# A one-core two-block model: the state-space layer's output projection laid between its last steps, a shorter softplus, first loads in three parts, and another order of routing and tail

## The chip, the cores and the metric

The kernel runs as one program on one core of a Trainium2 chip. The metric is the device time of an execution in microseconds (us). Four engines compute: TensorE (PE in the rows; weight loads are PEld), VectorE (DVE), ScalarE (ACT) and GpSimd (POOL). SyncE (SP) mostly issues DMA transfers.

## The reference

The input is one sequence of 256 tokens with 1024 features. Everything is float32. Only the parts around the change are shown.

```python
# block 1, layer 0: state-space mixer (32 heads in 8 groups, chunks of 64)
zxbcdt = u @ w_in;  z, xbc, dt_raw = split(zxbcdt);  xbc = silu(causal_conv(xbc) + conv_b)
dt = softplus(dt_raw + dt_bias);  a = -exp(a_log)
y = ssd_scan(xh * dt, dt * a, B, C) + xh * d_skip          # decays come from cumulative sums of dt*a
yg = (y * silu(z)) per group;  yg = yg * rsqrt(mean(yg**2) + eps) * norm_w
h = layer_norm(alpha * x + yg @ w_out)                      # the output projection
# then: squared-relu MLP, stick-breaking attention, MLP
# block 2: h = rms_norm(x, norm1_w) * (1 + sc1) + sh1;  x = x + g1 * token_mixer(h)   (softplus again, 8 columns)
h = rms_norm(x, norm2_w) * (1 + sc2) + sh2
comb = top-1 group of 4, top-2 experts of 8 in it           # routing over 32 experts
y = sum over experts of comb_e * (silu(h @ w_gate_e) * (h @ w_up_e)) @ w_down_e
x = x + g2 * y
return rms_norm(x, final_norm_w)
```

## The kernel before

The 256 tokens are two halves `m` of 128. Every large product is made of three matmuls on operands that are split into a rounded high part and a low part (`whi`, `wlo` for weights, `yh`, `yl` for activations). A weight comes by DMA in blocks of 1 MB (`wraw`); `wsplit` makes `whi` on ACT (L207) and `wlo` on DVE, now and then on POOL (L208). All matmuls of the helper `mm` stand under its one line, L233, so they are told apart by tiles. A scheduler orders the instructions of each engine, except inside `manual_schedule`, where the order of the code holds.

**State-space layer** (`mamba`). For each of 8 groups `g`, `proj(g)` makes the projections (tile `pj`), and `ssd(g)` is a generator of steps: `cb`, `xt` and `xdt`; two steps of decay weights (tile `bc`, read back by a DMA from `csd`); `spread`, which starts the next group's `bc` DMA; then `yp` on TensorE, `yz` on DVE (L474), `yz*Zg` on POOL (L476), the square on ACT and a sum `Zg` on POOL (L479); then `ss` on TensorE, `rr` on DVE (L485) and a power on POOL (L486); then `rb` on TensorE, `yz` on DVE (L492), `yh` on ACT and `yl` on DVE (L494). Steps of group g-1 and g-2 run between the projections of group g. Group 7 has no projections behind it. The output projection follows: 8 blocks `b` of `w_ao` (tile `acc`, four PSUM banks, 24 matmuls for each block). Block b needs the `yh`, `yl` of group b alone. Six blocks are issued in `phase_mamba`, the last two in `finish_ln`. In the code the blocks stand behind the last steps of groups 6 and 7, and the scheduler moves some of the matmuls up.

**Start.** `xT` and the first weight block come in four parts of 256 KB each; `dt_chain` computes softplus on 64 columns on DVE (L265 to L276), from which `cs`, the cumulative sums, and then `csT`, `csd` and the first `bc` follow.

**Routing** (`Router`). `logits(m)` (`lgp`), `route(m)` (a chain of small DVE operations from `lg` to `sel`), `split(m)` (the high and low part of the normalized rows, the low one by a POOL subtraction, L1474), `place(m)` (`pos`), `onehot`, `gather0` (`xgp`).

**Experts.** 96 blocks of 1 MB (`eraw`) stream through 18 buffers, issued by SP as buffers come free. For each k: `gu` (gate and up), `aT`, `down` (`py`, and its two parts `yh`, `yl`), `combine` (`yacc`). The last k ends the kernel: `grows` makes rows of g2 and of the final weight by 16 transposes (tile `rows`), then `final` scales, adds, squares, normalizes and writes the output.

Of the kernel before, what the change touches and what calls it, by code (L numbers as in the profile page):

```python
# [10 lines left out]
F32 = mybir.dt.float32  # L11
# [45 lines left out]
def lay(i):  # L57
# [60 lines left out]
    a["pv"] = pv  # L118
    a["c"] = f(i["c_2"])
# [40 lines left out]
def build(tc, A, out, dbg=None):  # L160
# [3 lines left out]
    with ctx:  # L164
# [97 lines left out]
        def softplus(dst, u, e, s_, q):  # L262
# [93 lines left out]
        def phase_mamba():  # L356
            with tc.tile_pool(name="mamba", bufs=2, reuse_waits="tile") as work:
                with tc.tile_pool(name="psm", bufs=4, space=PSUM, reuse_waits="tile") as psm:
                    yh, yl = mamba(work, psm)
                    acc = [pst("acc") for _ in range(4)]  # L360
                    for b in range(6):
                        tm(acc, wsplit(A["w_ao"][b]), yh, yl, 2 * b, b == 0, False)
                    return finish_ln(acc, [(wsplit(A["w_ao"][b]), yh, yl, 2 * b) for b in (6, 7)], 0)

        def mamba(work, psm):
# [10 lines left out]
            for c in range(0, 8, 2):  # L376
                cs, ws = slice(c, c + 2), slice(256 * c % 1024, 256 * c % 1024 + 512)
                with ExitStack() as es:
# [3 lines left out]
                    with tc.issue_after(x0):  # L382
                        tail = nc.sync.dma_start(raw0[:, 256 * c:256 * c + 512], A["w_a"][0][:, 256 * c:256 * c + 512]).ins
                S.activation(xh[:, cs], xT[:, cs], AF.Copy)
                V.tensor_tensor(xl[:, cs], xT[:, cs], xh[:, cs], op=OP.subtract)
                h, l = hl0[c // 4]
                S.activation(h[:, ws], raw0[:, 256 * c:256 * c + 512], AF.Copy)  # L387
                V.tensor_tensor(l[:, ws], raw0[:, 256 * c:256 * c + 512], h[:, ws], op=OP.subtract)
# [107 lines left out]
            rest = []  # L496
            for k, _ in enumerate(proj(0)):
                if k == 1:
                    dt_chain()
            rest.pop()()  # L500
            bcs = {(0, j): spread(work, 32, 2 * j, 2, 4) for j in range(2)}
# [3 lines left out]
            for g in range(1, 9):  # L505
                pr = proj(g) if g < 8 else iter(())
                sd = ssd(g - 1)
# [7 lines left out]
            for _ in range(3):  # L515
                next(old, 0)
            return yh, yl
# [4 lines left out]
        def brow(src, name, pool=None, q=nc.scalar):  # L522
            r = (pool or lnp_box[-1]).tile([128, D], F32, name=name, tag=name, bufs=1)
# [383 lines left out]
        def phase_mixer(keep, hT):  # L907
            gates = [keep.tile([128, 8, T], F32, name="gates", tag=t) for t in ("gA", "gB")]
            with wsp_pool(4, "right") as w_:
# [6 lines left out]
                with tc.tile_pool(name="mixo", bufs=2, reuse_waits="tile") as work, \  # L916
                        tc.tile_pool(name="pso", bufs=4, space=PSUM, reuse_waits="tile") as psd:
                    rt = mixer_out(keep, small, work, psd, *mhl[:2])
                    rt.early = mhl[2]
                    return raw2, rt  # L920
# [391 lines left out]
        def mixer_out(keep, small, work, psd, mh, ml):  # L1312
# [55 lines left out]
            def logits(m):  # L1368
                for c in range(8):
# [18 lines left out]
            rt.split(0, work, "hr")  # L1388
            add(1, 0, t)
            wo(1, 1, range(4))  # L1390
            rt.place(0)
            turn(1, 0, t)
            add(1, 1)

            def last(pool):
                junk = pool.tile([128, 512], F32, name="junk", tag="oc", bufs=1)
                turn(1, 1, junk)
                logits(1)
                route(1)
                rt.split(1, pool, "oT")  # L1400
# [6 lines left out]
        class Router:  # L1407
            def __init__(self, keep, bl):
# [17 lines left out]
                V.tensor_scalar(pn[:, 2:3], pn[:, 1:2], -2.0, 1.0, op0=OP.mult, op1=OP.add)  # L1426
                V.scalar_tensor_tensor(pn[:, 3:4], pn[:, 1:2], -64.0, pn[:, 0:1], op0=OP.mult, op1=OP.add)
                self.r, self.hs = [None, None], [None, None]
# [38 lines left out]
            def split(self, m, pool, tag):  # L1467
                h = self.hs[m]
# [384 lines left out]
```

## Time and profile before

| | before |
|---|---|
| median of 3 runs | 1240.29 us (1238.09 to 1243.02) |
| the profiled execution | 1241.94 us, span 1240.2 us |
| TensorE busy | 1181.6 us (95%) |
| VectorE busy | 757.1 us (61%) |
| ScalarE busy | 554.4 us (45%) |
| GpSimd busy | 215.7 us (17%) |
| mean granted TensorE clock | 0.983 |
| read from HBM | 293.38 MB, 239 GB/s over the span |

The shares are means over stages with different limits. Starts in the rows below are counted from the start of the span.

### The profile page before, as it was taken

To read this page: it belongs to the slowest core of one execution; us is meant where nothing else is said; L and a number is where in the kernel's file an instruction comes from. 1 tells how busy PE (TensorE), PEld (TensorE's weight loads), DVE (VectorE), ACT (ScalarE), POOL (GpSimd) and SP (SyncE) were. 2 spreads that over 40 slices of the span, in tenths; PEclk is the share of its full clock that TensorE was granted. 3 is DMA by queue.
4 is the path that set the end of the run, shared out by engine and by line. 5 is a ranking of instruction groups with operands and counts; after the bars stand their busy time and mean duration, and the time that the engine had idled before them with its cause. 6 is when DMAs were issued, how large, how long until landed. Compare 5 with 4: busy or idle time off the path is not lost. (4 is left out here: it accounts for less than half of the span.)

```text
span 1240.2 us, 19177 instructions
## 1 busy us (share of the span) xinstructions
PE 1181.6 (95%) x7669; PEld 966.7 (78%) x7669; DVE 757.1 (61%) x1241; ACT 554.4 (45%) x910; POOL 215.7 (17%) x164
## 2 busy tenths in 40 slices
PE   8799996999999999999999998999999989999995
PEld 7799995889899889978999987998999853444332
DVE  5878877497777675559777766667455772111113
ACT  4577573354444455646544434554444431111112
POOL 3355543000000000000000043355431020000001
PEclk9899999999999999999999999899999999999998
DMA  8655634547887744324878753443325599999992
GB/s 325 220 187 196 221 128 146 206 175 282 311 312 285 253 170 170 137 101 158 330 282 300 276 201 118 163 170 103 103 69 204 232 388 407 421 422 421 421 421 108
DMA packets 47078, 295.84 MB, mean 239 GB/s; under 512 B 5256, under 2 KB 6533, under 8 KB 14469
## 3 DMA queue, kind: packets, MB, share of 16 engines
q1 hardware_dynamic: 41120, 277.91, 59.6%
q10 hardware_dynamic: 5860, 16.63, 3.9%
q8 instruction: 62, 1.02, 0.3%
q14 instruction: 36, 0.29, 0.1%
HBM read 293.38 MB, written 2.71 MB: 239 GB/s over the span
## 5 line engine op out<-in xcount | busy, mean ns | idle before, releaser
L208 DVE TENSOR_TENSOR wlo<-wraw,whi 128x1024 fp32r<-128x1024 f32 x240 | 303.1, 1278 | 146.4 <-ACT whi L207 145.5
L207 ACT ACTIVATE whi<-wraw 128x1024 fp32r<-128x1024 f32 x282 | 294.0, 1057 | 212.0 <-PE acc L233 65.4
L208 POOL TENSOR_TENSOR wlo<-wraw,whi 128x1024 fp32r<-128x1024 f32 x42 | 109.8, 2622 | 265.6 <-ACT whi L207 265.6
L233 PE MATMUL u<-hTh,whi 128*128 128x256 f32 x448 | 125.7, 281 | 0.0
L233 PE MATMUL u<-hTh,wlo 128*128 128x256 f32 x448 | 125.3, 280 | 0.0
L233 PE MATMUL u<-hTl,whi 128*128 128x256 f32 x448 | 125.2, 280 | 0.0
L233 PE MATMUL pj<-xh,whi 128*128 128x256 f32 x384 | 113.2, 295 | 6.4 <-ACT whi L387 5.3
L233 PE MATMUL gu<-eraw,xg 128*64 128x512 f32 x512 | 113.3, 595 | 1.1 <-PE xgp L233 0.6
L233 PE MATMUL acc<-whi,mh 128*128 128x512 f32 x288 | 113.8, 395 | 0.0
L233 PE MATMUL pj<-xh,wlo 128*128 128x256 f32 x384 | 110.6, 288 | 3.3 <-DVE wlo L208 3.2
L233 PE MATMUL acc<-whi,ml 128*128 128x512 f32 x288 | 112.7, 391 | 0.0
L233 PE MATMUL acc<-wlo,mh 128*128 128x512 f32 x288 | 112.3, 390 | 0.0
L233 PE MATMUL pj<-xl,whi 128*128 128x256 f32 x384 | 110.8, 289 | 0.3
L233 PE MATMUL pj<-hTh,whi 128*128 128x256 f32 x320 | 93.4, 292 | 0.0
L233 PE MATMUL pj<-hTh,wlo 128*128 128x256 f32 x320 | 91.1, 285 | 0.0
L233 PE MATMUL pj<-hTl,whi 128*128 128x256 f32 x320 | 91.0, 284 | 0.0
L233 PEld LDWEIGHTS gu<-eraw,xg 128*64 128x64 f32 x512 | 36.9, 137 | 66.7 <-issue 62.5
L233 PEld LDWEIGHTS u<-hTh,whi 128*128 128x128 f32 x448 | 84.1, 188 | 1.7 <-issue 0.6
L233 PEld LDWEIGHTS u<-hTl,whi 128*128 128x128 f32 x448 | 83.9, 187 | 1.1
L233 PEld LDWEIGHTS u<-hTh,wlo 128*128 128x128 f32 x448 | 84.4, 188 | 0.0
L233 PEld LDWEIGHTS pj<-xh,whi 128*128 128x128 f32 x384 | 75.3, 196 | 8.8 <-ACT whi L387 5.3
L233 PEld LDWEIGHTS pj<-xh,wlo 128*128 128x128 f32 x384 | 75.5, 197 | 3.9 <-DVE wlo L208 3.4
(450 smaller groups left out, 2386.6 us busy)
## 6 DMA issues: line engine op xcount, KB each, us to landing
wraw<-in_w_dram SPq DMA_DIRECT2D x64, 1024.0 KB, 5.0
eraw<-in_w_gu_dram SPq DMA_DIRECT2D x58, 1024.0 KB, 19.3
eraw<-in_w_dn_dram SPq DMA_DIRECT2D x30, 1024.0 KB, 19.8
wraw<-in_w_mod_dram SPq DMA_DIRECT2D x24, 1024.0 KB, 6.0
wraw<-in_w_a_dram SPq DMA_DIRECT2D x23, 1024.0 KB, 5.3
wraw<-in_w_ao_dram SPq DMA_DIRECT2D x8, 1024.0 KB, 5.0
wraw<-in_w_bg_dram SPq DMA_DIRECT2D x8, 1024.0 KB, 5.1
bc<-csd ACTq DMA_DIRECT2D x16, 384.0 KB, 5.7
```

What stands on the lines that cost most here:

```text
L207: his.append(S.activation(h, r[:, us], AF.Copy).ins)
L208: (G if u in pool else V).tensor_tensor(l, r[:, us], h, op=OP.subtract)
L233: return PE.matmul(o, a, b, start=start, stop=stop, skip_group_check=True).ins
```

## The change

Six edits are made at once.

1. `mamba` returns the unfinished generators of groups 6 (`old`) and 7 (`sd`), and `phase_mamba` runs their steps between halves of blocks, `unit(b, m)` with 12 matmuls each, in an order written by hand for TensorE.
2. `softplus` takes one operation for a step of its polynomial, not two: seven fewer in each of the two places.
3. The first loads come in parts of 2, 2 and 4 of the 8 chunks. The sums `cs` and the first `spread` are called from the loop of group 1, and the first steps of group 0 start one projection later.
4. `split` is gone: `high` writes the high part straight from ACT, `low` makes the low part by one DVE operation. `logits(1)` comes in two halves, `gather0` takes all high parts before the low ones.
5. g2 is multiplied in `down` (now `chunk`), which gets one DVE operation more on its way and reads g2 from a row loaded by DMA.
6. `grows` and the POOL additions are gone. The final weight is loaded by DMA behind the last expert weights. The last `down` comes in chunks of 512, 256 and 256 columns with the sums of the final norm between them, `combine(6)` is wholly ahead of it, and the second half of the output is issued by ACT.

```diff
-                    yh, yl = mamba(work, psm)
+                    yh, yl, old, sd = mamba(work, psm)
                     acc = [pst("acc") for _ in range(4)]
-                    for b in range(6):
-                        tm(acc, wsplit(A["w_ao"][b]), yh, yl, 2 * b, b == 0, False)
+                    hl = {}
+                    def unit(b, m):
+                        if b not in hl:
+                            hl[b] = wsplit(A["w_ao"][b])
+                        tm(acc, hl[b], yh, yl, 2 * b, b == 0, False, mt=(m,))
+                    with tc.manual_schedule(engines={PE.engine}):
+                        for step in (sd, (0, 0), sd, (0, 1), old, sd, (1, 0), sd, old, (1, 1), sd, (2, 0), (2, 1),
+                                     (3, 0), sd, (3, 1), (4, 0), sd, (4, 1), (5, 0), (5, 1)):
+                            unit(*step) if isinstance(step, tuple) else next(step, 0)
...
-            V.tensor_scalar(q, e, 1.0 / (2 * K + 1), 1.0 / (2 * K - 1), op0=OP.mult, op1=OP.add)
+            V.tensor_scalar(q, e, 1.0 / (2 * K + 1), None, op0=OP.mult)
             for k in range(K - 1, 0, -1):
-                V.tensor_tensor(q, q, e, op=OP.mult)
-                V.tensor_scalar(q, q, 1.0 / (2 * k - 1), None, op0=OP.add)
-            V.tensor_tensor(q, q, s_, op=OP.mult)
+                V.scalar_tensor_tensor(q, q, 1.0 / (2 * k + 1), e, op0=OP.add, op1=OP.mult)
+            V.scalar_tensor_tensor(q, q, 1.0, s_, op0=OP.add, op1=OP.mult)
...
-            for c in range(0, 8, 2):
+            for c, n in ((0, 2), (2, 2), (4, 4)):
...
                 for k in range(6):
                     next(pr, 0)
+                    if g == 1 and k == 0:
+                        rest.pop()()
+                        bcs.update({(0, j): spread(work, 32, 2 * j, 2, 4) for j in range(2)})
                     if k in (2, 4, 5):
                         next(old, 0)
-                    if k < 5:
+                    if k < 5 if g > 1 else k:
                         next(sd, 0)
...
-            def split(self, m, pool, tag):
-                h = self.hs[m]
+            def high(self, m):
                 for n in range(2):
                     ns = slice(n * 512, n * 512 + 512)
-                    t = pool.tile([128, 512], F32, name="hr", tag=tag)
-                    S.activation(t, h_t[:, m, ns], AF.Copy, scale=self.r[m])
-                    S.activation(h[:, 0, ns], t, AF.Copy)
-                    G.tensor_tensor(h[:, 1, ns], t, h[:, 0, ns], op=OP.subtract)
+                    S.activation(self.hs[m][:, 0, ns], h_t[:, m, ns], AF.Copy, scale=self.r[m])
+            def low(self, m):
+                for n in range(2):
+                    ns = slice(n * 512, n * 512 + 512)
+                    V.scalar_tensor_tensor(self.hs[m][:, 1, ns], h_t[:, m, ns], self.r[m], self.hs[m][:, 0, ns],
+                                           op0=OP.mult, op1=OP.subtract)
...
+                V.scalar_tensor_tensor(t, py, cw, self.rt.g2[:, o:o + w], op0=OP.mult, op1=OP.mult)
+                S.activation(yh, t, AF.Copy)
+                V.tensor_tensor(yl, t, yh, op=OP.subtract)
...
-                    S.activation(yh, py, AF.Copy, scale=cw)
-                    V.scalar_tensor_tensor(yl, py, cw, yh, op0=OP.mult, op1=OP.subtract)
...
+                    self.fw = brow(A["finr"], "fw", self.keep, nc.sync, "gA")
                     self.turn(15)
-                    self.combine(6, (0,))
-                    self.down(7)
-                    self.combine(6, (1,))
-                    self.combine(7)
+                    self.combine(6)
...
+                        for c, t in enumerate((("ohs", "eyl"), ("eyh", "eyl"), ("eyh", "oT"))):
+                            y.append(self.chunk(7, CH[c], t))
+                            if c:
+                                self.combine(7, (c - 1,))
+                                if fin:
+                                    fin.part(c - 1)
...
+            def part(self, c):
...
+                for m in range(2):
+                    y = self.yacc[2 * m + (o > 0)]
+                    V.tensor_tensor(x[:, m, cs], y[:, o % 512:o % 512 + w], h_t[:, m, cs], op=OP.add)
+                    f = self.work.tile([128, w], F32, name="xf", tag="oc", bufs=1)
+                    S.activation(f, x[:, m, cs], AF.Square, scale=D ** -0.5, accum_out=q[:, m, c:c + 1])
...
+            def close(self):
...
+                for m in range(2):
+                    V.tensor_reduce(q[:, m, 4:5], q[:, m, 0:4], axis=AX.X, op=OP.add)
+                    G.tensor_tensor(q[:, m, 5:6], q[:, m, 4:5], nhalf[:, 0:1], op=OP.pow)
+                    V.tensor_tensor(x[:, m, n0], x[:, m, n0], self.fw[:, n0], op=OP.mult)
+                    S.activation(x[:, m, n0], x[:, m, n0], AF.Copy, scale=q[:, m, 5:6])
+                    V.scalar_tensor_tensor(x[:, m, n1], x[:, m, n1], q[:, m, 5:6], self.fw[:, n1],
+                                           op0=OP.mult, op1=OP.mult)
+                    (nc.sync, nc.scalar)[m].dma_start(out_m(m), x[:, m])
```

TensorE at the end of the state-space layer, before (`acc_2501` to `acc_2504` are the four banks, the number of a `whi` tells the weight block apart, `ss` and `rb` are steps of group 6 first and of group 7 below):

```order
L449 MATMUL xt_2438<-ident_77,Xg_2252 128x128 x4
...
L233 MATMUL acc_2502<-wlo_2508,yh_146 128x512
L233 MATMUL ss_2453<-ones_82,Zg_2069 128x1 x2
...
L490 MATMUL rb_2466<-ident_77,rr_2456 128x128 x2
L233 MATMUL yp_2473<-bc_2330,xdt_2443 64x256 x2
...
L233 MATMUL ss_2488<-ones_82,Zg_2356 128x1 x2
...
L490 MATMUL rb_2494<-ident_77,rr_2491 128x128 x2
```

The `acc` matmuls between these rows are 5 ahead of the first `ss`, 8 from there to `rb`, none from `rb` to `yp`, 20 to the second `ss`, 3 to the second `rb`, and 78 behind it in this phase. The same place of the changed kernel:

```order
L460 MATMUL xt_2435<-ident_77,Xg_2243 128x128 x4
...
L234 MATMUL ss_2484<-ones_82,Zg_2060 128x1 x2
...
L501 MATMUL rb_2519<-ident_77,rr_2487 128x128 x2
...
L234 MATMUL yp_2538<-bc_2321,xdt_2440 64x256 x2
...
L234 MATMUL ss_2609<-ones_82,Zg_2347 128x1 x2
...
L501 MATMUL rb_2649<-ident_77,rr_2612 128x128 x2
```

Here the counts of `acc` are 24 ahead of the first `ss`, 12 to `rb`, 12 to `yp`, 36 to the second `ss`, 24 to the second `rb`, and 36 behind it. VectorE at the same place, before, from the decay weights `bc` of group 7 on:

```order
L459 TENSOR_TENSOR bc<-bc,cb 128x768
L485 TENSOR_SCALAR rr<-ss 128x2
L459 TENSOR_TENSOR bc<-bc,cb 128x768
L492 SCALAR_TENSOR_TENSOR yz<-yz,pv,rb 128x256 x2
L208 TENSOR_TENSOR wlo<-wraw,whi 128x1024
L494 TENSOR_TENSOR yl<-yz,yh 128x512
L474 SCALAR_TENSOR_TENSOR yz<-Xg,hd,yp 128x256 x2
L208 TENSOR_TENSOR wlo<-wraw,whi 128x1024 x2
L485 TENSOR_SCALAR rr<-ss 128x2
```

And after:

```order
L470 TENSOR_TENSOR bc<-bc,cb 128x768 x2
L209 TENSOR_TENSOR wlo<-wraw,whi 128x1024 x2
L496 TENSOR_SCALAR rr<-ss 128x2
L209 TENSOR_TENSOR wlo<-wraw,whi 128x1024
L503 SCALAR_TENSOR_TENSOR yz<-yz,pv,rb 128x256 x2
L505 TENSOR_TENSOR yl<-yz,yh 128x512
L209 TENSOR_TENSOR wlo<-wraw,whi 128x1024 x2
L485 SCALAR_TENSOR_TENSOR yz<-Xg,hd,yp 128x256 x2
L209 TENSOR_TENSOR wlo<-wraw,whi 128x1024 x2
L496 TENSOR_SCALAR rr<-ss 128x2
```

Two `wlo` now stand ahead of the first `rr`, and two more ahead of the `yz` of group 7. TensorE at the routing, before (`tp` are the transposes of the second half's rows, `pos` the places, `xgp` the gather):

```order
L233 MATMUL pos<-sel,iu 128x32
L233 MATMUL pos<-run,ones 128x32
L1355 MATMUL tp<-ident,h 128x128 x8
L233 MATMUL lgp<-wg,xT 128x40 x8
L233 MATMUL xgp<-oh,hs 128x256 x16
```

And after:

```order
L1367 MATMUL tp<-ident,h 128x128 x4
L234 MATMUL lgp<-wg,xT 128x40 x4
L234 MATMUL pos<-sel,iu 128x32
L234 MATMUL pos<-run,ones 128x32
L1367 MATMUL tp<-ident,h 128x128 x4
L234 MATMUL lgp<-wg,xT 128x40 x4
L234 MATMUL xgp<-oh,hs 128x256 x16
```

The first half's places moved behind the first four transposes and logits of the second half.

## Rows read from the trace of the kernel before

**Rows 1.** The page: rate of all transfers in 40 slices; DVE's low parts of weights.

```profile
GB/s 325 220 187 196 221 128 146 206 175 282 311 312 285 253 170 170 137 101 158 330 282 300 276 201 118 163 170 103 103 69 204 232 388 407 421 422 421 421 421 108
...
L208 DVE TENSOR_TENSOR wlo<-wraw,whi 128x1024 fp32r<-128x1024 f32 x240 | 303.1, 1278 | 146.4 <-ACT whi L207 145.5
```

**Rows 2.** Timeline of TensorE: start, length, instruction, [idle before, releaser].

```profile
195.10 0.48 PE L233 MATMUL acc<-whi,yh 128*128 128x512 f32 x1
...
199.95 0.61 PE L233 MATMUL ss<-ones,Zg 128*128 128x1 f32 x4 [3.44 <-POOL Zg L479]
...
206.02 0.40 PE L233 MATMUL acc<-whi,yl 128*128 128x512 f32 x1
...
210.15 0.39 PE L233 MATMUL acc<-whi,yl 128*128 128x512 f32 x1
212.73 0.60 PE L233 MATMUL ss<-ones,Zg 128*128 128x1 f32 x4 [2.19 <-POOL Zg L479]
...
215.28 0.69 PE L490 MATMUL rb<-ident,rr 128*128 128x128 f32 x2 [1.14 <-POOL rr L486]
...
220.46 0.63 PE L233 MATMUL acc<-whi,yl 128*128 128x512 f32 x1
```

**Rows 3.** Busy time by window: length, PE, PEld, DVE, ACT, POOL, PEclk, DMA share, GB/s.

```profile
215.00:220.00 5.00, 4.72 (x12) 3.78 (x13) 1.22 (x3) 1.43 (x2) 0.23 (x1) 0.50 0.59 213
```

**Rows 4.** Timeline of GpSimd at the end of the state-space layer.

```profile
200.89 0.71 POOL L486 TENSOR_TENSOR rr<-rr,nhalf 128x2 f32<-128x2 f32 x1 [1.00 <-DVE rr L485]
207.96 3.26 POOL L476 TENSOR_TENSOR yz<-yz,Zg 128x512 f32<-128x512 f32 x1 [6.36 <-DVE yz L474]
...
213.68 1.55 POOL L486 TENSOR_TENSOR rr<-rr,nhalf 128x2 f32<-128x2 f32 x1 [1.00 <-DVE rr L485]
```

**Rows 5.** Timeline of TensorE in group 1: the sums and the first `yp`.

```profile
34.74 0.41 PE L233 MATMUL cs<-sm,ic 128*128 128x32 f32 x2 [1.81 <-DVE sm L284]
...
58.14 0.87 PE L233 MATMUL yp<-bc,xdt 128*64 128x256 f32 x8 [1.34 <-DVE bc L459]
```

**Rows 6.** Timeline of VectorE: one of the softplus operations on 64 columns.

```profile
29.96 0.20 DVE L273 TENSOR_SCALAR sm<-sm 128x64 f32<-128x64 f32 x1
```

**Rows 7.** Timeline, second block's mixer: a softplus operation on VectorE, and TensorE's wait.

```profile
778.09 0.17 DVE L273 TENSOR_SCALAR sm<-sm 128x8 f32<-128x8 f32 x1
...
790.48 0.49 PE L301 MATMUL csT<-ident,csr 128*4 128x128 f32 x3 [2.51 <-DVE csr L296]
```

**Rows 8.** Timeline of the second half's routing: VectorE, GpSimd and TensorE.

```profile
1004.06 0.15 DVE L1440 CAST sc<-idx 128x1 f32<-128x1 uint32 x1
1004.25 0.24 DVE L1441 TENSOR_SCALAR le<-gid,sc 128x32 f32<-128x32 f32 x1
...
1005.28 1.02 DVE L1447 CAST sc<-idx 128x2 f32<-128x2 uint32 x1
1006.34 1.20 DVE L1448 TENSOR_SCALAR s<-iot,sc 128x32 f32<-128x32 f32 x1
...
1005.01 2.48 POOL L1474 TENSOR_TENSOR hs<-hr,hs 128x512 fp32r<-128x512 f32 x2 [1.97 <-ACT hs L1473]
...
1007.97 0.38 PE L233 MATMUL pos<-sel,iu 128*128 128x32 f32 x2 [2.81 <-DVE sel L1449]
```

**Rows 9.** Busy time by window (columns as in rows 3): the dip, and the last weights.

```profile
1015.00:1020.00 5.00, 5.00 (x26) 1.58 (x22) 3.32 (x20) 0.41 (x2) 1.23 (x2) 1.00 0.84 274
...
1214.00:1216.00 2.00, 0.89 (x7) 0.23 (x3) 0.90 (x2) 0.77 (x2) 0.00 (x0) 1.00 0.49 187
```

**Rows 10.** Timeline of the tail: TensorE, and VectorE's last operation.

```profile
1204.72 1.09 PE L1802 MATMUL rows<-ident,modc 128*128 128x128 f32 x8
...
1207.40 7.09 PE L233 MATMUL gu<-eraw,xg 128*64 128x512 f32 x32 [0.20 <-ACT rows L1803]
...
1217.27 7.09 PE L233 MATMUL py<-eraw,aT 128*64 128x512 f32 x32
...
1233.33 0.75 DVE L1580 SCALAR_TENSOR_TENSOR x<-x,fq,rows 128x512 f32<-128x512 f32 x1 [0.44 <-POOL fq L1597]
```

More of the change, by code (lines that the diff above doesn't have):

```diff
@@ L496, in mamba @@
             rest = []
+            bcs = {}
             for k, _ in enumerate(proj(0)):
-                if k == 1:
+                if k == 2:
                     dt_chain()
-            rest.pop()()
-            bcs = {(0, j): spread(work, 32, 2 * j, 2, 4) for j in range(2)}
             with tc.issue_after(his[-1]):
@@ L1366, in turn, with logits @@
                 G.tensor_tensor(q[:, m, 3:4], q[:, m, 2:3], nhalf[:, 0:1], op=OP.pow)
-            def logits(m):
-                for c in range(8):
+            def logits(m, cs=range(8)):
+                for c in cs:
                     mm(lgp[:, m * 40:m * 40 + 40], xT[:, c, m * 128:m * 128 + 128], wg[:, c], c == 0, c == 7)
@@ L1387, in mixer_out @@
             t = route(0, lambda: scaled(1, 0))
-            rt.split(0, work, "hr")
+            rt.high(0)
             add(1, 0, t)
             wo(1, 1, range(4))
-            rt.place(0)
             turn(1, 0, t)
             add(1, 1)
+            logits(1, range(4))
+            rt.place(0)
             def last(pool):
@@ L1397, in last @@
                 turn(1, 1, junk)
-                logits(1)
+                logits(1, range(4, 8))
+                rt.low(0)
                 route(1)
-                rt.split(1, pool, "oT")
             rt.last = last
@@ L1552, in moe @@
             exp.onehot(0, 1)
+            rt.low(1)
             exp.gather0(1)
@@ L1560, in moe @@
             cnti = exp.run(0, yacc)
-            final(exp, work, yacc)
             rv = nc.values_load(cnti[0:1, 0:1], min_val=0, max_val=T)
@@ new lines, in moe, with __init__ @@
+                with tc.manual_schedule(engines={V.engine, S.engine, G.engine}):
+                    fin = Final(exp, work, yacc)
+                    for c in range(3):
+                        fin.part(c)
+                    fin.close()
+        CH = ((0, 512), (512, 256), (768, 256))
+        class Final:
+            def __init__(self, exp, work, yacc):
+                self.fw, self.yacc = exp.fw, yacc
+                self.work = work
+                self.x = work.tile([128, 2, D], F32, name="x", tag="xgB", bufs=1)
+                self.q = work.tile([128, 2, 6], F32, name="fq", tag="fq", bufs=1)
+                V.memset(self.q[:, :, 3:4], 1e-6)
+            def part(self, c):
+                x, q = self.x, self.q
+                o, w = CH[c]
+                cs = slice(o, o + w)
+                for m in range(2):
+                    y = self.yacc[2 * m + (o > 0)]
[3 more added lines that the diff above has]
+            def close(self):
+                x, q = self.x, self.q
+                n0, n1 = slice(0, 512), slice(512, 1024)
+                for m in range(2):
+                    V.tensor_reduce(q[:, m, 4:5], q[:, m, 0:4], axis=AX.X, op=OP.add)
[5 more added lines that the diff above has]
+                    (nc.sync, nc.scalar)[m].dma_start(out_m(m), x[:, m])
@@ L1657, in gather0 @@
                     self.new_xg(0)
-                for d2 in range(4):
-                    self.gather(0, self.banks[d2], d2, m)
-                    if m:
-                        self.drain(0, self.banks[d2], d2, (0, 1))
+                for part in range(2):
+                    for d2 in range(4):
+                        self.gather(0, self.banks[d2], d2, m, (part,))
+                        if m and part:
+                            self.drain(0, self.banks[d2], d2, (0, 1))
             def prep(self, q):
@@ L1741, in combine @@
+            def down(self, k):
+                self.ys[k] = [self.chunk(k, (512 * n, 512), ("eyh", "eyl")) for n in range(2)]
             def combine(self, k, ns=(0, 1)):
-                y = self.ys[k]
                 oT = self.oTs[k // 2][:, k % 2]
                 for n in ns:
+                    (o, w), *y = self.ys[k][n]
                     for m in range(2):
+                        p = self.yacc[2 * m + (o > 0)][:, o % 512:o % 512 + w]
                         for part in range(2):
-                            mm(self.yacc[2 * m + n], oT[:, m * 128:m * 128 + 128], y[n][part],
+                            mm(p, oT[:, m * 128:m * 128 + 128], y[part],
```

116 lines of the change are left out of this document (44 added, 72 removed).

## The prediction

> **What bounds the kernel now.** The table shows TensorE busy for 95% of the span, so what it loses is found in its idle places, and I went through the rows that name a wait in brackets. They stand in five places. One is the end of the state-space layer: TensorE idles 3.44, 2.19 and 1.14 us there [rows 2], and the window from 215 to 220 was granted a clock of 0.50, the lower of its two levels, 1.2 GHz, after these idle stretches [rows 3]. One is the start, with 1.81 us at `cs` and 1.34 us at the first `yp` [rows 5]. One is the mixer of the second block, 2.51 us at `csT` [rows 7], and one the routing, 2.81 us at `pos` [rows 8]. The fifth is the tail, where TensorE is followed by a chain on VectorE to 1234.1 [rows 10]. In the seven slices of 31 us from 992 to 1209 the transfers run at 388 to 422 GB/s [rows 1]: the experts are bound by the weight stream. The three slices before have 69, 204 and 232: the stream comes up only as the mixer's work ends and its buffers come free. So what is gained ahead of it should reach the end, and inside the stream only an earlier start, a filled dip or a shorter tail counts.
>
> **The end of the state-space layer.** TensorE starts the output projection at 195.10. Between 206.02 and 210.15 there are 18 equal steps without a wait: 0.229 us for an `acc`. From 195.10 to 220.46 TensorE started 47 of them [rows 2], which is 10.8 us of work. Beside them it ran two `ss`, two `rb` and one `yp`. A row's length holds the filling of the pipe too (an `acc` has 0.39, but starts every 0.229, so 0.17 too much): two `ss` at 0.61 give 0.9, two `rb` at 0.69 or less 0.8, and `yp`, two runs like the eight matmuls of 0.87 in [rows 5], 1.4. That is 13.9 of 25.4 us. 11.5 us are lost, 6.8 of them in the three waits and the rest at half clock, and the window row says that the half clock lasts a little beyond 220 [rows 3]; I put the loss at 11.7.
>
> Does the new order remove all of it? I walk through it with these durations. TensorE has 24 `acc` first and reaches the first `ss` at 195.10 + 24 x 0.229 = 200.6. Its operand was there at 199.95 [rows 2], and nothing ahead of it has moved: no wait. `rr` now stands behind two `wlo` of VectorE at 1.28 each [rows 1]. Before, the power started 0.94 after `ss` and took 0.71 [rows 4]. With the first decay products ending about 200.2, `rr` comes at about 202.7 and the power ends at 203.4. TensorE reaches `rb` after 12 `acc`, at 200.6 + 0.45 + 2.75 = 203.8. The margin is 0.4; with the other power's 1.55 [rows 4] there is a wait of 0.4. Then 12 `acc` lead to `yp` at 207.0, and its 1.4 and 36 `acc` to the second `ss` at 216.6. Before, `yp` began at about 204.1 (behind `ss` at 199.95, 8 `acc` at half clock, 12 of which took 4.72 in [rows 3], and `rb`), the product on GpSimd 3.9 later, and `ss` 4.8 after the product's start [rows 2, 4]. With the same delays `Zg` is ready at 215.7: a margin of 0.9. The second `rb` came 2.6 after `ss`, and 24 `acc` (5.5 us) now cover it. I take -11.7. It can hardly be more than -12.5 (whole work against whole time); if both margins break, a wait of 1 to 2 us with the half clock behind it leaves -7.5.
>
> **Start.** The wait for `cs` (1.81) goes, since 24 projections (0.115 each, half of an `acc` with half the columns) stand ahead of it now, and softplus is shorter by seven operations of 0.20 [rows 6]; the operation that stays in each step reads the same two tiles as the multiplication did, and I take it to be as long. But `csT`, from which the decays go through DRAM to `yp`, stands behind 33 more projections, 3.8 us, and TensorE reaches the first `yp` only 24 projections later, 2.8 us less the 1.81 removed. So the wait of 1.34 at `yp` may grow by up to 2.8, or stay, as softplus also frees VectorE 1.4 us earlier for the convolutions. The three larger loads save two issues and let chunks 4 and 5 wait for 6 and 7. I take 0 together, from -2.5 to +2.5.
>
> **Mixer.** Seven operations of 0.17 go from VectorE's queue [rows 7], ahead of the convolutions and the `csr` on which TensorE waits 2.51: -1.2. The ends are 0 (a weight's split on GpSimd is last instead) and -4, the whole wait and the half clock behind it.
>
> **Routing.** While GpSimd subtracts (2.48 for two), VectorE's CAST takes 1.02, not 0.15, and its TENSOR_SCALAR 1.20, not 0.24 [rows 8]. Without the subtraction 1.8 us go from the chain to `sel`. Two new operations of 512 columns, 0.75 each by the nearest row [rows 10], come ahead of that chain, beside the second half's transposes and logits. I take -1.4: 0 if both lie on the path and hide nothing else, -2.8 if the whole wait goes. It counts for the stream, for the buffers are freed by `gu` behind it: from 1015 to 1020 the stream falls to 274 GB/s [rows 9], against 421 a loss of 1.75 us, and more at lower depth behind it.
>
> A rule of the Trainium skill (GPSIMD Engine Reference, 8. Key points) says that GpSimd shares its SBUF interfaces with VectorE and collides with instructions that have two SBUF inputs, or run in a 2-port mode. The rows of the subtraction agree. It speaks against the first edit: `wlo` has two such inputs, and four of them now flank the product on GpSimd, which would by the rule stay at its 3.26 or grow, where the sum takes it as it was.
>
> **Down and tail.** The added VectorE operation of `chunk` (0.75, as [rows 10]) and the load of g2 are hidden by the stream; VectorE has little else there. Without that cover each `down` would cost 1.5. In the tail the 16 transposes and their copies go: `gu` starts at 1204.72, not 1207.40, 2.7 earlier [rows 10]. Four `yacc` (0.9) come ahead of the last `py` instead of behind its first half, so that it starts at 1215.5. The last weights have landed by then: the window from 1214 to 1216 moves 187 GB/s, so the stream ended about 1214.9 [rows 9], which caps the gain at 2.4 unless the stream ends earlier too. From `py` to the end of the last VectorE operation it took 16.8 before; now one more operation and two more steps of a chain stand between `py` and `yacc`, for 256 columns in the last chunk, while products with g2 and sums on GpSimd go. I call that even: -1.9 with 0.15 for the shorter last `yacc`, between -3 and +0.5.
>
> **Sum.** -11.7 + 0 - 1.2 - 1.4 - 1.9 = -16.2, from 1241.94 to 1225.7. The profiled execution was 1.65 above the median of the runs shown; against the median that is 1224.
>
> **Rivals.** *A, the stalls move.* If the two `wlo` ahead of the `yz` of group 7 start late, for their ACT halves wait for buffers that the first blocks free, the second `ss` is 2.6 later than 215.7, TensorE waits 1.7 us and runs some 5 us at half clock, where 12 `acc` took 4.72 [rows 3], not 2.75: +2 more, 3.7 in all. With the `rb` of group 6 also late, -11.7 becomes about -7.5: 1228 to 1232. For it speak the small margins, against it that 36 `acc` lie between. The rule on the shared interface ends in the same place by another way: if the product takes another 1 to 2 us beside `wlo`, the margin of 0.9 is used up and the time is 1225 to 1227; it has a chance of 0.2 within the forecast and A, as a product with two `wlo` beside it took 3.26 already before.
>
> *B, more goes than I count.* The mixer's whole wait with its half clock (-4), the start's two waits (-2) and the whole routing wait: 1216 to 1219. Against it: `csr` waits for other things on VectorE as well.
>
> *C, the gain is hidden.* If the expert stream were set by memory from further ahead, and not released by the mixer, 14 of the 16 us would turn into waits for weights: about 1237. The low rate of the slices just before it [rows 1] speaks against it.
>
> *D, slower.* Its place is the chain from `cs` to the first `yp`, 23.4 us in [rows 5]. If the later `csT` and a DMA that now meets the weight loads make `bc` L us later than TensorE can bridge, the price is L and about L/2 for the half clock. It decides from L = 11 on; a chain of 23 us would have to grow by half. Then 1247 or more.
>
> **How the numbers follow.** Forecast 0.57 (1219.5 to 1228), A 0.20, B 0.13, C 0.06, D 0.04. From 1216 to 1232 leaves out C, D and edges of A and B, some 0.15. 0.5% is 6.2 us, about what a measurement of this kernel can tell from no change: faster (below 1234.1) is all but D and most of C, 0.91; same 0.06; slower 0.03.
>
> **What would show it.** Right: the `acc` of the output projection evenly spaced at 0.23 from 195 on, no wait over 0.5 us at `ss` or `rb`, and the last `py` starting at about 1201 (1217.3 less all but 0.15 of the sum). No subtraction on GpSimd at the routing, and a CAST of 0.15. Wrong: a bracket of over 1 us with GpSimd at the second `ss`, a granted clock under 0.9 in the window from 200 to 225, a wait of more than 4 us at the first `yp`, or waits for expert weights longer by what the front gained.

## Result, and the profile after

The changed kernel took 1225.68 us (median of 4 runs, 1218.55 to 1227.33), the kernel before 1239.19 us (4 runs, 1237.23 to 1243.02) beside it: a ratio of 0.9873, 95% interval 0.9841 to 0.9905. The profiled execution took 1226.38 us. The forecast was 1224, and 1225.7 for a profiled execution.

The page of the changed kernel, engines and the rate of transfers in 40 slices (for [rows 1]):

```profile
PE 1172.4 (96%) x7673; PEld 962.0 (79%) x7673; DVE 768.1 (63%) x1251; ACT 549.9 (45%) x907; POOL 203.5 (17%) x158
...
GB/s 328 232 130 218 196 191 186 192 159 325 308 317 276 231 177 168 139 103 157 334 285 299 264 227 132 169 173 104 99 75 176 210 419 416 421 421 421 421 421 178
```

A single total hides where time went, so I cut the profiled executions at the same events: A, start to the first `acc` of the output projection; B, first to last of its `acc`; C, to the mixer's `csT`; D, to the issue of the first of the ten expert loads that SyncE sends in a row (two single blocks went out 29 us ahead of it); E, to the first `gu`; F, to the first `py` of the last `down`; G, to the end of the last VectorE operation; H, the rest of the execution's time. A to F are differences of two starts in the timelines.

| us | A | B | C | D | E | F | G | H | total |
|---|---|---|---|---|---|---|---|---|---|
| before | 195.10 | 59.77 | 535.61 | 182.94 | 39.93 | 203.92 | 16.81 | 7.86 | 1241.94 |
| changed | 198.89 | 48.51 | 534.83 | 182.73 | 37.51 | 200.57 | 16.18 | 7.16 | 1226.38 |
| difference | +3.79 | -11.26 | -0.78 | -0.21 | -2.42 | -3.35 | -0.63 | -0.70 | -15.56 |

**Stage B.** TensorE at the end of the state-space layer, changed (for [rows 2]):

```profile
198.89 0.48 PE L234 MATMUL acc<-whi,yh 128*128 128x512 f32 x1
...
204.48 0.50 PE L234 MATMUL ss<-ones,Zg 128*128 128x1 f32 x4
...
208.13 0.43 PE L501 MATMUL rb<-ident,rr 128*128 128x128 f32 x2 [0.27 <-POOL rr L497]
...
211.26 1.52 PE L234 MATMUL yp<-bc,xdt 128*64 128x256 f32 x16
...
221.08 0.50 PE L234 MATMUL ss<-ones,Zg 128*128 128x1 f32 x4
227.04 0.38 PE L501 MATMUL rb<-ident,rr 128*128 128x128 f32 x2
```

Only one of the four narrow steps shows a wait, of 0.27. The window that held the half clock in [rows 3] is at the full level, as are all of 5 us from 198 to 228:

```profile
215.00:220.00 5.00, 5.00 (x24) 4.10 (x23) 1.60 (x2) 2.75 (x3) 1.64 (x2) 1.00 0.91 307
```

GpSimd there (for [rows 4]): the second product took 1.29, not 3.26, as it fell between VectorE's `wlo` (two until 213.68, the next at 218.25). So `Zg` was there at 217.38, 3.7 us ahead of TensorE's second `ss`.

```profile
206.52 1.55 POOL L497 TENSOR_TENSOR rr<-rr,nhalf 128x2 f32<-128x2 f32 x1 [2.57 <-DVE rr L496]
214.61 1.29 POOL L487 TENSOR_TENSOR yz<-yz,Zg 128x512 f32<-128x512 f32 x1 [6.53 <-DVE yz L485]
```

**Stages C and E.** TensorE at the mixer's `csT` (for [rows 7]); then the second half's routing, VectorE and TensorE (for [rows 8]); then the window of the dip (for [rows 9]), taken as there from about 1.6 us behind the first `gu`:

```profile
782.23 0.49 PE L301 MATMUL csT<-ident,csr 128*4 128x128 f32 x3 [1.70 <-DVE csr L296]
...
997.29 0.17 DVE L1461 CAST sc<-idx 128x2 f32<-128x2 uint32 x1
997.49 0.24 DVE L1462 TENSOR_SCALAR s<-iot,sc 128x32 f32<-128x32 f32 x1
...
998.17 0.38 PE L234 MATMUL pos<-sel,iu 128*128 128x32 f32 x2 [1.49 <-DVE sel L1463]
...
999.81 2.14 PE L234 MATMUL xgp<-oh,hs 128*128 128x256 f32 x16 [1.04 <-DVE oh L1640]
...
1004.00:1009.00 5.00, 5.00 (x26) 1.58 (x22) 3.29 (x20) 0.41 (x2) 1.22 (x2) 1.00 1.00 410
```

The waits fell from 2.51 to 1.70 and from 2.81 to 1.49, and 274 GB/s became 410. Behind the wait of 2.81 the clock had fallen (0.70 from 1010 to 1015), and the second gather `xgp` had taken longer than the 2.14 above:

```profile
1009.62 3.64 PE L233 MATMUL xgp<-oh,hs 128*128 128x256 f32 x16 [1.05 <-DVE oh L1620]
```

**Stages F and G.** The tail, TensorE and VectorE (for [rows 10]):

```profile
1195.67 3.65 PE L234 MATMUL gu<-eraw,xg 128*64 128x512 f32 x14 [1.35 <-DMA eraw<-in_w_gu_dram]
...
1203.04 5.38 PE L234 MATMUL py<-eraw,aT 128*64 128x512 f32 x32
...
1218.47 0.75 DVE L1617 SCALAR_TENSOR_TENSOR x<-x,fq,fw 128x512 f32<-128x512 f32 x1 [0.43 <-POOL fq L1614]
```

No `rows` stands ahead of the last `gu`; in its place TensorE waits 1.35 for weights.

**Stage A** is the one that got longer. TensorE in the first groups of the changed kernel (for [rows 5]):

```profile
49.51 0.81 PE L301 MATMUL csT<-ident,csr 128*32 128x128 f32 x3 [4.46 <-DVE csr L296]
...
105.60 0.69 PE L501 MATMUL rb<-ident,rr 128*128 128x128 f32 x2 [3.69 <-POOL rr L497]
```

The wait for `cs` is gone. There are new ones of 4.46 at `csT` and 3.69 at the `rb` of group 1 (groups are counted from 0, as in the code; the expectations below call this place the third group). The first comes from VectorE: `csr`, which `csT` needs, stands there behind two `wlo` that run beside two of GpSimd and take 6.64, not the 2.36 of two alone (at 203.95).

```profile
41.22 6.64 DVE L209 TENSOR_TENSOR wlo<-wraw,whi 128x1024 fp32r<-128x1024 f32 x2
...
41.00 5.78 POOL L209 TENSOR_TENSOR wlo<-wraw,whi 128x1024 fp32r<-128x1024 f32 x2 [2.92 <-ACT whi L208]
```

What the waits are worth is a question for the experiments.

### The profile page after: what moved, and what is told of

Same layout as the page of the kernel before. It is cut to its first block, busy times and chain, and to the rows that moved or that the text cites. A ratio compares the mean times of both kernels' runs of the same rounds, so it can differ in the third digit from the quotient of the medians.

```text
span 1224.7 us, 19176 instructions
## 1 busy us (share of the span) xinstructions
PE 1172.4 (96%) x7673; PEld 962.0 (79%) x7673; DVE 768.1 (63%) x1251; ACT 549.9 (45%) x907; POOL 203.5 (17%) x158
```

## Experiments

Times are medians, each beside runs of the kernel before on the same chip; ratios are to those, with 95% intervals. Stages are those of the table.

**A copy, and the start.** The first three runs ask whether the start edit costs the 3.8 us of stage A. `e0_again` is an unchanged copy. `e1_old_start` has the first loads, the sums and the first steps as before, `e2_new_loads_old_sums` keeps the three loads and has all hunks but the first (in both, `dt_chain` is called one projection earlier again, too):

```diff
-            for c, n in ((0, 2), (2, 2), (4, 4)):
+            for c in range(0, 8, 2):
...
+            rest.pop()()
+            bcs = {(0, j): spread(work, 32, 2 * j, 2, 4) for j in range(2)}
...
-                    if g == 1 and k == 0:
-                        rest.pop()()
-                        bcs.update({(0, j): spread(work, 32, 2 * j, 2, 4) for j in range(2)})
...
-                    if k < 5 if g > 1 else k:
+                    if k < 5:
```

> The changed kernel once more, as it is, for comparison with the others on the same chip. Theory S (the first output-projection matmul came 3.8 us later, at 198.9 instead of 195.1, because of the start's edit) expects it at 198 to 200 again, the csT wait on VectorE near 4.5 us, and a time near 1225. Rival V (this delay is a chance of one execution, and the start's edit costs nothing) expects the first output-projection matmul anywhere from 194 to 199.

> The changed kernel with the start as before: four parts of loads, sums and first decay products ahead of group 1's loop, first steps of group 0 as before; the shorter softplus stays. Theory S expects the first output-projection matmul at 195 or a little earlier, no csT wait of 4 us, and 3 to 5 us less than the changed kernel, near 1221. Rival V expects the time of the changed kernel, within 1.5 us.

> The changed kernel with the loads in three parts kept, but the sums, the first decay products and the first steps of group 0 where they were. If the later place of the sums and of csT is what costs (theory S, by the order), it is as fast as with the whole old start, 3 to 5 us below the changed kernel. If the larger last part of the loads costs (rival L), it stays within 1.5 us of the changed kernel, and the second TensorE wait at the start is at 10.3 and not 7.5.

Measured: 1224.54 (0.9890, 0.9857 to 0.9922), 1224.34 (0.9886, 0.9858 to 0.9913) and 1224.51 (0.9882, 0.9858 to 0.9907). Stage A was 199.91, 194.74 and 196.85 in the profiles, but the medians are equal, as rival V had it. So the 3 to 5 us of theory S are not seen; each interval reaches 3 to 4 us to either side, and a smaller loss by the start is neither shown nor ruled out.

**The projection's order.** `e3_old_projection` is the changed kernel with the projection behind the last steps, `e4_projection_alone` the kernel before with the order by hand and nothing else. The diff is that of `e3_old_projection`; the other is its reverse:

```diff
-                    with tc.manual_schedule(engines={PE.engine}):
-                        for step in (sd, (0, 0), sd, (0, 1), old, ...):
-                            unit(*step) if isinstance(step, tuple) else next(step, 0)
+                    for b in range(6):
+                        tm(acc, wsplit(A["w_ao"][b]), yh, yl, 2 * b, b == 0, False)
```

> The changed kernel with the output projection behind the last steps, in the scheduler's order, as before; everything else as changed. The theory that the hand-written order is worth 11.3 us (its length from first to last matmul fell from 59.8 to 48.5) expects 10 to 12 us more than the changed kernel, near 1236, with waits of 3.4 and 2.2 us at ss and a granted clock near 0.5 behind them. The rival that most of it came from elsewhere expects under 5 us more.

> The kernel before with the hand-written order of the output projection alone. The theory that the order is worth 11 us, and that nothing behind it takes them back, expects 10 to 12 us less than before, near 1228, and 48 to 49 us from the first to the last matmul of the projection. The rival that half of it turns into waits for weights in the MLP or in the experts expects 5 to 6 us less.

Measured: `e3_old_projection` 1235.5 (0.9975, 0.9952 to 0.9998), 11 above the copy, with stage B 58.82 and the waits of [rows 2] back:

```profile
196.06 0.61 PE L234 MATMUL ss<-ones,Zg 128*128 128x1 f32 x4 [3.45 <-POOL Zg L481]
...
208.74 0.61 PE L234 MATMUL ss<-ones,Zg 128*128 128x1 f32 x4 [2.12 <-POOL Zg L481]
211.30 0.69 PE L492 MATMUL rb<-ident,rr 128*128 128x128 f32 x2 [1.14 <-POOL rr L488]
```

`e4_projection_alone` took 1226.93 beside 1236.8: the medians differ by 9.9 us, the ratio (0.9939, 0.9917 to 0.9961) gives 7.5. Its stage B is 48.29, 11.5 less than before. B is 48.05 to 48.53 in all twelve profiles with the order by hand, 58.8 and 59.8 in the two without: the order is worth its 11 us in its stage, alone or with the rest. Why the whole time of the lone edit shows less stays open. The start, below, scatters by as much, and D was 3.0 more than before's in its profile, with two more stretches at the lower clock.

**The low parts on GpSimd.** `e5_low_on_gpsimd` puts the subtraction of the routing back:

```diff
-                    V.scalar_tensor_tensor(self.hs[m][:, 1, ns], h_t[:, m, ns], self.r[m], self.hs[m][:, 0, ns],
-                                           op0=OP.mult, op1=OP.subtract)
+                    G.tensor_tensor(self.hs[m][:, 1, ns], self.hr[m][n], self.hs[m][:, 0, ns], op=OP.subtract)
```

> The changed kernel with the routing's low parts subtracted on GpSimd again (two ACT copies and a subtraction for each half row, as before), in the new order. If the collision of GpSimd with VectorE carried the routing's gain, the time from the first expert load to the first gu rises from 37.5 by 1 to 2.5, a CAST or TENSOR_SCALAR of route takes about 1 us, and the kernel 1 to 2.5 us longer. If the new order carries it, the stretch stays within 0.6 of 37.5.

Measured: 1230.74 (0.9950, 0.9929 to 0.9972); stage E 41.65, not 37.5. VectorE and GpSimd, and the window around them:

```profile
994.16 0.60 DVE L1462 CAST sc<-idx 128x2 f32<-128x2 uint32 x1
994.80 1.21 DVE L1463 TENSOR_SCALAR s<-iot,sc 128x32 f32<-128x32 f32 x1
...
993.44 2.53 POOL L1492 TENSOR_TENSOR hs<-hr,hs 128x512 fp32r<-128x512 f32 x2 [1.97 <-ACT hs L1487]
...
994.00:999.00 5.00, 3.13 (x14) 2.76 (x14) 3.33 (x9) 0.39 (x2) 1.97 (x2) 0.50 1.02 424
```

These two operations take 1.4 longer (1.8 in [rows 8]). That is a part of the 4.1. Counted from the first expert load, the second half's transposes begin 0.9 later than in the changed kernel (TensorE waits 1.38 for `h` of VectorE, not 0.38) and its `pos` 2.4 later, which fits the expected 1 to 2.5. The rest is the clock: it was at its lower level from about 991, so ahead of this chain, to 1004, and the second `xgp` took 3.75, not 2.14. The edit need not be the only cause of that: `e1_old_start`, `e2_new_loads_old_sums` and `e6_transposes_back` have the changed routing, fell to the lower level there for a shorter time, and have an E of 38.6; the other profiles with that routing have 37.4 to 37.6.

**The transposes, and softplus.** `e6_transposes_back` adds 16 transposes ahead of the last `gu`; `e8_long_softplus` takes back edit 2:

```diff
+                        if k == 7:
+                            self.grows()
...
-                V.scalar_tensor_tensor(q, q, 1.0 / (2 * k + 1), e, op0=OP.add, op1=OP.mult)
+                V.tensor_tensor(q, q, e, op=OP.mult)
+                V.tensor_scalar(q, q, 1.0 / (2 * k - 1), None, op0=OP.add)
```

> The changed kernel with the 16 transposes and four copies put back ahead of the last gu (their result is not used). The prediction's term, by which TensorE is the bound there, expects the last py 2.7 us later and the kernel 2.7 us longer. The rival that the weight stream is the bound there (gu waited 1.35 and py 0.80 for weights in the changed kernel) expects at most 1 us.

> The changed kernel with the longer softplus in both places. The prediction's term expects the wait at the second mixer's csT 0.8 to 1.2 us longer (2.5, not 1.7), the kernel about 1 us longer, and nothing lost at the start. The rival that softplus is covered in both places expects no difference at csT beyond 0.3.

Measured: `e6_transposes_back` 1226.88 (0.9916, 0.9886 to 0.9946), stage F 203.02, which is 2.45 more (200.1 to 201.4 in the other profiles with the changed tail). The median alone would not tell, as its interval holds the copies' ratios of 0.9890, 0.9908 and 0.9914. The whole last `gu` of 32 now follows without the wait of 1.35:

```profile
1187.39 1.09 PE L1836 MATMUL rows<-ident,modc 128*128 128x128 f32 x8
...
1190.42 7.09 PE L234 MATMUL gu<-eraw,xg 128*64 128x512 f32 x32
```

`e8_long_softplus` 1229.65 (0.9929, 0.9901 to 0.9957): the wait at the mixer's `csT` is 2.48 again, and stage C 535.63, 0.80 more. C is 535.60 to 535.63 in the three profiles with the long softplus and 534.7 to 534.9 in the eleven with the short one. That settles the mixer; the median's further distance lies in A (199.23) and D (185.87).

**What the start's scatter is.** In the profiles up to here stage A of kernels with the same start was 191.2 to 199.9. I first held GpSimd's queue for the cause, where the selections from the `bc` of group 3, when that lands late, stand ahead of the power of group 1, and took it away: `e9_power_first` gives the steps from `ss` to the power priority.

```diff
+                es_ = ExitStack()
+                es_.enter_context(tc.high_priority())
                 p = pacc("ss")
...
                 G.tensor_tensor(r, r, nhalf[:, 0:2], op=OP.pow)
+                es_.close()
```

> The changed kernel, with ss, rr and the power of every group given priority, so that at the third group two wlo and half of the selections that wait for bc no longer stand ahead of the power on GpSimd. Theory Q (GpSimd's queue behind a late bc is what made TensorE wait 2.9 to 3.7 us at rb there, with the half clock behind it): no wait over 1 us at that rb, the output projection begins at 189 to 194 and not at 199 to 200, whenever bc lands; the median is 2 to 5 us below the copy's, where the copy shows the late bc in most of its executions. Rival R (a late bc delays TensorE by itself, or the start scatters for another reason): a wait of 2 us or more at yp, ss or rb of the first groups, and a beginning at 194 to 200. Neither expects more than 1 us from the first acc to the last py.

> A copy of the changed kernel, for its own scatter on this chip: the median within 4 us of 1225; the first acc at 190 to 200, late (199 to 200) where the third group's bc takes 5 us or more from its issue to its selections, and early (190 to 194) where it takes about 4.

Measured: `e9_power_first` 1231.43 (0.9936, 0.9913 to 0.9959), the copy 1228.22 (0.9914, 0.9886 to 0.9943). The wait at `rb` went and others came, at `ss`, of 2.24 (at 92.55) and of 3.68, and A was 201.92:

```profile
118.15 1.01 PE L234 MATMUL ss<-ones,Zg 128*128 128x1 f32 x4 [3.68 <-POOL Zg L490]
```

Theory Q fell: without that wait the start is no shorter. The copy's profiled execution took 1217.33, with A 191.43 and the `bc` of group 3 selected 3.5 us after its issue (early, as expected), so that two executions of one code can be laid side by side. In group 2 one weight block's two halves of `wlo` run on VectorE and GpSimd; the first result's profile, then the copy's:

```profile
77.24 2.42 POOL L209 TENSOR_TENSOR wlo<-wraw,whi 128x1024 fp32r<-128x1024 f32 x1
...
77.27 3.48 DVE L209 TENSOR_TENSOR wlo<-wraw,whi 128x1024 fp32r<-128x1024 f32 x1
```

```profile
75.32 1.23 DVE L209 TENSOR_TENSOR wlo<-wraw,whi 128x1024 fp32r<-128x1024 f32 x1
...
75.63 3.19 POOL L209 TENSOR_TENSOR wlo<-wraw,whi 128x1024 fp32r<-128x1024 f32 x1
```

In all 13 profiles that have this pair, the one that starts first keeps its pace, and the other is held. With GpSimd first by 0.03 us, VectorE takes 2.25 us more. GpSimd's product behind it starts at 87.34, not 84.20 (TensorE was 2.2 us behind the copy ahead of the pair already), and takes 3.34, not 2.21. The profiles fall in two sets without overlap: VectorE first (`e3_old_projection`, `e4_projection_alone`, `e5_low_on_gpsimd`, `e6_transposes_back`, `e10_copy`) with A 190.4 to 193.3; GpSimd first (before, changed, `e0_again`, `e1_old_start`, `e2_new_loads_old_sums`, `e8_long_softplus`, `e9_power_first`) with A 194.7 to 201.9. The last pair of runs is a kernel that gives both halves to VectorE, and a copy:

```diff
-                hl = wsplit(A["w_a"][3 * g + 2], (1,) if g else (0, 1))
+                hl = wsplit(A["w_a"][3 * g + 2], () if g == 2 else (1,) if g else (0, 1))
```

> The changed kernel with one weight block's low parts (the third block of group 2) made wholly by VectorE; in the profiles seen so far its two halves start within 0.3 us of each other on VectorE and GpSimd. Theory P (whichever engine starts first keeps its speed: VectorE first 1.23, GpSimd first 3.2 to 3.5 on VectorE, and in the second case the output projection begins at 199 to 200, not at 191 to 193): the VectorE wlo at 74 to 81 take 1.25 or less each, the projection begins at 189 to 194 in every execution, and the median is 2 to 6 us below the copy's, with a narrower scatter. Rival R (the start scatters for another reason): the projection begins at 194 to 200 all the same, or the median is within 2 us of the copy's.

> A copy of the changed kernel on the same chip, for the comparison: median 1224 to 1229, with a scatter of 10 us or more. Theory P: the first acc at 190 to 194 if VectorE's wlo at 74 to 81 starts before GpSimd's and takes 1.23, at 199 to 200 if GpSimd's starts first and VectorE's takes 3.2 to 3.5. Rival R: no such split.

Measured: `e11_race_removed` 1223.08 (1222.19 to 1224.29, 5 runs; 0.9889, 0.9847 to 0.9932), the copy 1224.94 (1220.38 to 1232.02, 12 runs; 0.9908, 0.9879 to 0.9937). Both low parts keep their pace in the first:

```profile
74.03 1.21 DVE L209 TENSOR_TENSOR wlo<-wraw,whi 128x1024 fp32r<-128x1024 f32 x1
76.11 1.21 DVE L209 TENSOR_TENSOR wlo<-wraw,whi 128x1024 fp32r<-128x1024 f32 x1
```

Its A is 193.63, and its five runs lie within 2.1 us where the copy's twelve span 11.6 (and the six of `e2_new_loads_old_sums`, which has the pair, 4.1). The copy's profile had GpSimd first by 0.28, 3.23 on VectorE, and A 197.57: the split held, below the band expected. The medians differ by 1.9, under the 2 us that I had set, so a gain is not shown, and no version here clearly beats the changed kernel.

Nor is the pair of `wlo` shown to be the root. Before and `e4_projection_alone` have one code there, the `wlo` in the other order and an A of 195.10 and 190.36, but 4.4 us of the 4.7 were lost ahead of the pair: `ss` of group 0, ahead of it, starts at 74.83 and 70.47, that of group 1 at 94.98 and 90.63. And the executions of the changed code part earlier, by TensorE's clock. Windows of the start, the first result, then `e10_copy` (columns as in [rows 3], the clock third from the end):

```profile
18.00:22.00 4.00, 3.84 (x33) 3.64 (x33) 1.55 (x4) 1.86 (x2) 3.01 (x2) 1.00 0.79 289
34.00:38.00 4.00, 2.63 (x12) 2.42 (x13) 3.69 (x5) 4.00 (x7) 2.41 (x1) 0.74 0.00 0
50.00:54.00 4.00, 4.00 (x23) 3.81 (x22) 4.00 (x10) 1.20 (x2) 0.00 (x0) 0.63 0.57 240
```

```profile
18.00:22.00 4.00, 3.84 (x23) 3.63 (x23) 2.60 (x6) 1.92 (x5) 3.76 (x3) 0.67 0.97 369
34.00:38.00 4.00, 4.00 (x36) 4.00 (x36) 3.73 (x5) 3.31 (x7) 2.02 (x1) 1.00 0.26 49
46.00:50.00 4.00, 2.62 (x12) 2.31 (x12) 3.67 (x10) 1.81 (x3) 0.00 (x0) 0.59 0.94 330
```

Where the lower level comes at 18 to 26, TensorE has no long wait near 34 and keeps the full level there (`e3_old_projection`, `e5_low_on_gpsimd`, `e6_transposes_back`, `e10_copy`, `e11_race_removed`: A 191.2 to 193.6). Where those windows are at the full level, it waits 1.95 for a `whi` near 35 and the lower level comes behind that (changed, `e0_again`, `e9_power_first`, `e12_copy`: A 197.6 to 201.9). Both kinds have it once more near `csT`, and by the first `yp` the first result is only 2.5 us behind the copy (62.92 and 60.47). `e8_long_softplus`, with the lower level at 22 to 26 and A 199.23, fits neither. So the profile of `e11_race_removed` was of the early kind anyway.

Half and more of the difference arises later, between the `ss` of group 1 and that of group 2. There ACT issues the DMA of group 3's `bc` and GpSimd makes selections from it, the first result, then `e10_copy`; then TensorE's `rb` of group 1 in `e11_race_removed`:

```profile
90.83 0.81 ACTq L309 DMA_DIRECT2D bc<-csd  x2
97.87 2.09 POOL L312 TENSOR_SCALAR_AFFINE_SELECT bc<-bc 128x256 f32<-128x256 f32 x4 [5.71 <-DMA bc<-csd]
```

```profile
86.56 0.81 ACTq L309 DMA_DIRECT2D bc<-csd  x2
90.09 0.77 POOL L312 TENSOR_SCALAR_AFFINE_SELECT bc<-bc 128x256 f32<-128x256 f32 x2 [2.01 <-DMA bc<-csd]
```

```profile
101.74 0.43 PE L501 MATMUL rb<-ident,rr 128*128 128x128 f32 x2 [1.90 <-POOL rr L497]
```

In the ten profiles with the new start this DMA goes out 0.15 us after GpSimd's product of group 1 ends, behind the square on ACT that waits for it; before, it went out ahead of the product (at 84.31, the product at 86.58). And where the `bc` is selected 3.5 to 4.1 us after its issue (`e3_old_projection`, `e5_low_on_gpsimd`, `e6_transposes_back`, `e10_copy`), the two `ss` are 20.5 to 20.9 us apart; where it takes 5.7 to 7.0 (changed, `e0_again`, `e8_long_softplus`, `e11_race_removed`, `e12_copy`), 24.0 to 26.7. `e11_race_removed`, without the pair, is among the second. So the pair of `wlo` and the late `bc` go together in the copies, but no run shows which of them, if either, makes the start late. Why the DMA sometimes takes longer, and why the clock is sometimes lower at 18, stays open.

## Why the prediction was right

That the total came so close was luck: two misses of 3 to 4 us, in opposite directions, met in it. The start took 3.8 more than put, the rest gave 3.2 more. The largest term was right in mechanism and size. By its terms:

- **State-space end, -11.7:** -11.26, with the waits gone as in the walk. `e3_old_projection` gives it back. `ss` and the second `rb` came without a wait. The first `rb` waited 0.27: its power took 1.55, the branch for which the walk had a wait of 0.4 and not a margin of 0.4. At the second `ss` the margin was 3.7, not 0.9, as the product took 1.29. This is the step on which most hung. Rival A did not come.
- **Mixer, -1.2:** -0.78, and +0.80 in `e8_long_softplus`. The wait fell by 0.8, not by the whole 1.2 of the seven operations.
- **Routing, -1.4, and tail, -1.9:** E fell by 2.42, F by 3.35, G by 0.63, H by 0.70, 7.1 in all where 3.3 were put. Of E, 1.34 are the path, the size of the term: counted from the first expert load, `pos` came at 33.21, not 34.55. The rest is mostly the second `xgp` at the full clock, which the term did not have. Of F, 2.5 belong to this profile of before: `e4_projection_alone`, with the old routing and tail, has 201.44 and not 203.92, as in before 26 matmuls of the last `py` but one took 7.92, partly at the lower clock, and 6.22 there. Against `e4_projection_alone`, E, F and G fell by 2.55, 0.87 and 0.62, so 4.0. The transposes are worth 2.45 (`e6_transposes_back`), near the 2.4 at which the weights were said to cap them; 1.35 of wait for weights stands where they were. "Even" was wrong for G by 0.5. H was not priced: the output goes out on two queues, issued at 1217.43 and 1219.30, where before one took both; that this is its cause is not shown.
- **Start, 0 (-2.5 to +2.5):** +3.79 in the profile, outside the ends. The waits at the first `yp` did not grow (0.81 in all, 1.34 and 0.78 before), as one branch had it. The walk counted what TensorE has ahead of `csT`, not what VectorE has ahead of `csr` (two `wlo` in 6.64), where TensorE waited 4.46 (and 5.95 in `e10_copy`, whose A is 191.43); and it stopped at the first `yp`, ahead of the 3.69 at the `rb` of group 1. How much of the +3.79 is the edit's is not shown, as one code scatters by 8 us: A is 190.4 to 196.9 in the four profiles with the old place of the sums, and 191.2 to 199.9 in the nine with the new one and no edit of the power. The medians of `e0_again` and `e1_old_start` show no loss.
- **Down's operation, 0:** F holds no loss; it was not tried alone.
- **Rivals.** B did not come: waits of 1.70 and 1.49 are left in the mixer and the routing, and the start grew. C fell: the 11 us of stage B are the 11 of the medians of `e3_old_projection` and the copy. D fell: it needed 11 us and more, and A rose by 3.8.

The sum without the start was -16.2 and is -19.35, 2.5 of it the slower `py` of this profile of before; with the start, -15.56.

The rule of the Trainium skill on the shared interface (GPSIMD Engine Reference, 8. Key points) did not bite where I weighed it, since no `wlo` ran while the product did (1.29). It did ahead of `csT`, in group 2 and in `e5_low_on_gpsimd`, as the rows above show. The Trainium skill (Perfetto Trace Analysis, Optimizing Scalar/DVE Operations) says that moving work between GpSimd and VectorE might not help, as they share a read port; the 1.21 to 3.48 of `wlo` agrees with the sharing. Here the routing's subtraction did gain from the move.

## What to carry to other kernels

Put work that is ready between the steps of a dependent chain, and count from the trace how many pieces of it each step needs: here 24, 12, 12, 36 and 24 matmuls covered every step, worth 11 us. Cut profiles at the same events before you compare them: a total can be right while two of its stages are each off by 4 us. Where an order is moved, walk through every engine's queue ahead of the moved step, not TensorE's alone: here `csr` came behind two `wlo`. Where two engines get halves of one job at the same moment, look at which starts first in several executions.

## What the runs showed of the hardware that I had not expected

- Two `wlo` of the same shape started within 0.3 us on VectorE and GpSimd take 1.23 and 3.19, or 3.48 and 2.42: the later one is held. A difference of 0.03 us decided it.
- The start of one code takes 191.4 or 197.6 to 199.9 us (`e10_copy` against changed, `e0_again`, `e12_copy`). Half and more of that arises where the `bc` of group 3 lands late; a lower clock at 18 to 26, where TensorE would wait soon after, cost nothing that A shows.
- After a wait of 1.70 at the mixer's `csT` the clock of the changed kernel fell: 0.66 from 782 to 787. In `e1_old_start`, after one of 1.73, it stayed at 1.00, first row from 778:

```profile
782.00:787.00 5.00, 4.77 (x29) 4.73 (x30) 0.86 (x4) 1.85 (x3) 2.38 (x1) 0.66 0.29 122
```

```profile
778.00:783.00 5.00, 5.00 (x45) 4.97 (x44) 0.55 (x1) 2.47 (x5) 2.39 (x1) 1.00 0.28 98
785.00:790.00 5.00, 5.00 (x45) 5.00 (x44) 2.36 (x6) 2.98 (x8) 2.75 (x2) 1.00 0.59 246
```

Directly behind the wait it fell in four of the eleven profiles with waits of 1.67 to 1.79, and in all three with 2.48 to 2.64. Stage D, behind it, is 181.1 and 181.3 in the two copies (`e10_copy`, `e12_copy`) that kept the full level for 60 us behind it, and 182.7 to 186.0 in all others.
